# Winograd convolution: the weights' load moved from SyncE's to ScalarE's hardware queue

## The chip, the cores and the metric

The kernel runs on one core of a Trainium2 chip. The metric is the device time of one execution in microseconds (us), told as the median of several runs. Beside it a profiled execution gives a span (first to last instruction, some 1.8 us shorter than the time) and a trace of every instruction and every DMA packet. In the lines of the profile PE is TensorE's matrix unit and PEld its loading of weights, DVE is VectorE, ACT ScalarE, POOL GpSimd, SP SyncE; a q behind the name is the engine's sequencer, which issues transfers, and L48 is line 48 of the kernel.

## The reference

A 3x3 convolution with padding 1, in float32: 16 images of 64 channels and 64 x 64 pixels, 128 output channels.

```python
x_pad = np.pad(x, ((0, 0), (0, 0), (1, 1), (1, 1)), mode='constant')
for b in range(batch):
    for co in range(c_out):
        for ci in range(c_in):
            for kh in range(3):
                for kw in range(3):
                    output[b, co] += weight[co, ci, kh, kw] * x_pad[b, ci, kh:kh+h, kw:kw+w]
```

In are 16.8 MB of images and 0.295 MB of weights, out are 33.5 MB.

## The kernel before

Two images form a pair, one on each half of the partitions; there are 8 pairs. All loads and all stores go out on SyncE's queue, in this order: weights, pair 0 in four pieces, pairs 1 to 6 whole, then the stores pair by pair, with the load of the last pair slipped in after the third store. The weights are cast, transposed on TensorE and combined before the first image matmul can run.

```python
    w_raw = const.tile([CO, CI * 9], F32)
    nc.sync.dma_start(w_raw, w_flat)
    cuts = [(0, 18), (18, 34), (34, 50), (50, 64)]
    # ... cut: buffers of load(p) ...
        for lo, hi in cuts if p == 0 else [(0, H)]:
            keep(
                nc.sync.dma_start(
                    xf[p][:, lo:hi, :], x_rows[128 * p : 128 * p + 128, lo:hi, :]
                )
            )
    # ... cut ...
    for p in range(LATE):            # LATE = 7
        load(p)
    # ... cut ...
    keep(nc.vector.tensor_copy(w16, w_raw))
    # ... cut: 18 transposing matmuls of w16 into wps[1], wps[2], wps[0] ...
    keep(nc.scalar.copy(wrow(G1), wps[1]))
    sums(nc.vector, 0, xf[0], 0, RB)
    # ... cut: main loop over pairs and blocks of 8 row pairs ...
            parts = {3: (0, 64)} if p < NP - 1 else {1: (0, 32), 3: (32, 64)}
            if blk in parts:
                lo, hi = parts[blk]
                keep(nc.sync.dma_start(
                    out_pairs[p, :, :, lo:hi, :],
                    ots[p].rearrange("p b j i c -> p b (j i) c")[:, :, lo:hi, :],
                ))
                if p == 2:
                    load(LATE)
```

## Time and profile before

| | before |
|---|---|
| median time | 127.7 us (127.53 to 127.8) |
| span of the profiled execution | 126.6 us |
| PE, VectorE, ScalarE busy | 106.0, 84.3, 65.5 us |
| DMA packets | 50.77 MB, mean 401 GB/s |
| last store issued | 112.84 us |

Two more views matter for this change. First, the page's DMA issues (what, queue, count, KB each, median us from issue to landing):

```profile
xf<-in_x_dram SPq DMA_DIRECT2D x1, 576.0 KB, 4.9
...
w_raw<-in_weight_dram SPq DMA_DIRECT2D x1, 288.0 KB, 3.0
```

Second, the timeline of the head (start us, us, engine, line, operation, and in brackets the idle time before it and what ended it):

```profile
3.72 0.46 DVE L88 CAST w<-w_raw 128x576 f16<-128x576 f32 x1 [3.72 <-DMA w_raw<-in_weight_dram]
...
4.90 0.48 ACT L118 CAST Wt<-wp 128x384 f16<-128x384 f32 x1 [2.88 <-PE wp L116]
...
6.06 0.69 DVE L98 TENSOR_TENSOR ss<-xf 128x512 f16<-128x512 f32 x1 [1.88 <-DMA xf<-in_x_dram]
...
6.80 1.47 PE L174 MATMUL acc<-ss,Wt 64*128 64x512 f16 x6 [1.24 <-DVE ss L98]
```

The reader is to see that the first weight row is ready at 4.90 + 0.48 = 5.38 us, and that the first matmul then waits until 6.80 for the image's row sum: in the kernel before, the image is the later of the two.

### The profile page before, as it was taken

Reading aid. Unit: us, or ns where it says so; the run is one execution under the profiler, and the core shown is the slowest. Engines: PE = TensorE matmul, PEld = TensorE weight load, DVE = VectorE, ACT = ScalarE, POOL = GpSimd, SP = SyncE. Lnnn points to the kernel's source line nnn. Section 1 sums busy time; section 2 is a strip of 40 time slices with the busy share of each in tenths; the row PEclk is TensorE's granted clock in tenths of the full one; section 3 lists DMA queues with packets and bytes.
Section 4 is the critical chain, followed back from the end, with each engine's and each line's share of the span. In section 5 each row is a group of like instructions: output and inputs, shape, how many; then the busy total and the mean of one; then the engine's idle time right before and its main releaser. Section 6 shows DMA issues by size and latency. Waiting matters only on the chain.

```text
span 126.6 us, 2424 instructions
## 1 busy us (share of the span) xinstructions
PE 106.0 (84%) x978; PEld 55.8 (44%) x978; DVE 84.3 (67%) x135; ACT 65.5 (52%) x98; POOL 33.3 (26%) x22
## 2 busy tenths in 40 slices
PE   0489999999999999999999999999999999920000
PEld 0334555555555555555555555555555555500000
DVE  0287777777777777777877787778777877760000
ACT  4283999998789876666333333336666333300000
POOL 2000395930780075007600660068000000000000
PEclk9999999999999999999999999999999999999555
DMA  4999999999999999999999999999999999999940
GB/s 116 322 422 435 424 430 419 450 419 424 430 440 437 409 442 409 435 435 419 440 414 435 424 419 435 430 435 430 414 430 445 424 424 419 432 417 424 432 184 13
DMA packets 4186, 50.77 MB, mean 401 GB/s; under 512 B 336, under 2 KB 336, under 8 KB 976
## 3 DMA queue, kind: packets, MB, share of 16 engines
q1 hardware_dynamic: 4176, 50.63, 95.1%
q8 instruction: 7, 0.11, 0.3%
q14 instruction: 3, 0.02, 0.0%
HBM read 17.07 MB, written 33.55 MB: 400 GB/s over the span
## 4 chain that ended last, share of the span: by engine, by line
PE 82%; DMA 4%; DVE 2%; issue 1%; DVEq 0%; SPq 0%
PE acc L174 82%; DMA xf<-in_x_dram 4%; DVE ot L194 1%; DVE ss L98 1%; DVEq L230 0%; DVE ot L197 0%; SPq L48 0%; DVEq L194 0%
## 5 line engine op out<-in xcount | busy, mean ns | idle before, releaser
L174 PE MATMUL acc<-xs,Wt 64*128 64x504 f16 (+3 forms) x768 | 88.9, 378 | 0.0
L174 PEld LDWEIGHTS <-Wt 64*128 64x128 f16 x960 | 54.7, 95 | 50.9 <-issue 3.3
L194 DVE TENSOR_TENSOR ot<-acc,ut 128x512 f32<-128x512 f32 x64 | 41.2, 686 | 21.9 <-PE acc L174 18.2
L188 ACT COPY ut<-acc 128x512 f32<-128x512 f32 x64 | 34.4, 590 | 39.7 <-issue 35.2
L197 DVE TENSOR_TENSOR ot<-acc,ut 128x512 f32<-128x512 f32 x64 | 41.1, 683 | 0.2 <-PE acc L174 0.2
L75 ACT CAST xs<-xf 128x1024 f16<-128x1024 f32 (+2 forms) x30 | 30.9, 1065 | 0.7 <-DMA xf<-in_x_dram 0.7
L174 PE MATMUL acc<-ss,Wt 64*128 64x504 f16 (+1 forms) x192 | 27.1, 384 | 1.2 <-DVE ss L98 1.2
L98 POOL TENSOR_TENSOR ss<-xs 128x1024 f16<-128x1024 f16 x8 | 16.8, 2124 | 30.8 <-PE acc L174 30.8
L98 POOL TENSOR_TENSOR ss<-xf 128x1024 f16<-128x1024 f32 x6 | 14.1, 2363 | 23.5 <-DMA xf<-in_x_dram 14.9
L116 PE MATMUL wp<-ident,w 128*64 128x128 f16 x18 | 1.3, 329 | 4.2 <-DVE w L88 4.2
L98 DVE TENSOR_TENSOR ss<-xf 128x512 f16<-128x512 f32 x4 | 2.8, 689 | 2.8 <-DMA xf<-in_x_dram 2.8
L116 PEld LDWEIGHTS <-w 128*64 128x64 f16 x18 | 1.1, 211 | 4.2 <-DVE w L88 4.2
L88 DVE CAST w<-w_raw 128x576 f16<-128x576 f32 x1 | 0.5, 460 | 3.7 <-DMA w_raw<-in_weight_dram 3.7
L118 ACT CAST Wt<-wp 128x384 f16<-128x384 f32 x1 | 0.5, 479 | 2.9 <-PE wp L116 2.9
L75 POOL CAST xs<-xf 128x896 f16<-128x896 f32 x2 | 1.9, 926 | 0.0
L118 ACT ACT_TABLE_LOAD x1 | 1.3, 1283 | 0.7 <-PEq L219 0.7
L123 ACT CAST Wt<-wp 128x384 f16<-128x384 f32 x1 | 0.5, 479 | 0.5 <-DVE Wt L121 0.5
L120 DVE TENSOR_TENSOR Wt<-wp,Wt 128x384 f16<-128x384 f32 x1 | 0.6, 550 | 0.0
L121 DVE TENSOR_TENSOR Wt<-wp,Wt 128x384 f16<-128x384 f32 x1 | 0.5, 547 | 0.0
L124 ACT CAST Wt<-wp 128x384 f16<-128x384 f32 x1 | 0.5, 485 | 0.0
masks.py:199 POOL TENSOR_SCALAR_AFFINE_SELECT ident<-ident 128x128 f16<-128x128 f16 x1 | 0.3, 295 | 0.1
masks.py:197 POOL MEMSET ident<- 128x128 f16 x1 | 0.2, 205 | 0.3 <-POOLq L219 0.3
(4 smaller groups left out, 0.4 us busy)
## 6 DMA issues: line engine op xcount, KB each, us to landing
out_dram<-ot SPq DMA_DIRECT2D x7, 4096.0 KB, 21.1
xf<-in_x_dram SPq DMA_DIRECT2D x7, 2048.0 KB, 21.2
out_dram<-ot SPq DMA_DIRECT2D x2, 2048.0 KB, 13.6
xf<-in_x_dram SPq DMA_DIRECT2D x2, 512.0 KB, 6.1
xf<-in_x_dram SPq DMA_DIRECT2D x1, 576.0 KB, 4.9
xf<-in_x_dram SPq DMA_DIRECT2D x1, 448.0 KB, 7.2
w_raw<-in_weight_dram SPq DMA_DIRECT2D x1, 288.0 KB, 3.0
```

The source lines that it names most:

```text
L75: keep(copy(xs[p][:, lo:hi, :], xf[p][:, lo:hi, :]))
L88: keep(nc.vector.tensor_copy(w16, w_raw))
L98: eng.tensor_add(ss[p][:, lo : lo + n, :], v[:, lo : lo + n, 0, :], v[:, lo : lo + n, 1, :])
L116: nc.tensor.matmul(wp[q : q + 64, k * CO : k * CO + CO], w16[:, t::9], ident)
L118: keep(nc.scalar.copy(wrow(G1), wps[1]))
L120: keep(nc.vector.tensor_sub(wrow(G21), wps[2], wrow(G1)))
L121: keep(nc.vector.tensor_sub(wrow(G01), wps[0], wrow(G1)))
L123: keep(nc.scalar.copy(wrow(G0), wps[0]))
L174: nc.tensor.matmul(tiles[b2][:, lo - j0 : hi - j0, c_lo:c_hi], Wt[p0 : p0 + 64, wi, kw, :], rhs, start=i == 0, stop=i == n - 1,)
L188: keep(nc.scalar.copy(ut, U[b2]))
L194: nc.vector.tensor_add(ots[p][:, b2, j0 : j0 + RB, 0, :], A[b2], us[b2])
L197: nc.vector.tensor_add(ots[p][:, b2, j0 : j0 + RB, 1, :], Bt[b2], us[b2])
```

## The change

Its intent: SyncE's first instruction becomes the first image load, which therefore is issued earlier, and the weights come beside it on the other hardware queue. The whole diff:

```diff
     w_raw = const.tile([CO, CI * 9], F32)
-    nc.sync.dma_start(w_raw, w_flat)
+    nc.scalar.dma_start(w_raw, w_flat)
```

## The prediction

> **What bounds the kernel now.** I read four views, in this order: the 40 slices of the page, the chain that ended last, the DMA issues asked one by one, and the DMA view of the last 11.6 us. The slices come first, because they show which resource has no idle slice. The three rows are tenths of VectorE busy, tenths of DMA busy, and GB/s; a slice is 126.6 / 40 = 3.165 us.
>
> ```profile
> DVE  0287777777777777777877787778777877760000
> DMA  4999999999999999999999999999999999999940
> GB/s 116 322 422 435 424 430 419 450 419 424 430 440 437 409 442 409 435 435 419 440 414 435 424 419 435 430 435 430 414 430 445 424 424 419 432 417 424 432 184 13
> ```
>
> The reader is to see that the transfers fill every slice but the first and the last two, at some 428 GB/s (the table of stretches has 427 to 429 in each 20 us from 5 to 105 us), and that they go on for nearly three slices after VectorE has stopped. The page counts 50.77 MB; 50.77 MB / 428 GB/s = 118.6 us of a span of 126.6. So the DMA engines are the candidate, although the chain of waits puts 82% on the matmuls. The chain's own rows show why that is no contradiction (start us, us, what):
>
> ```profile
> 0.74 0.39 SPq L48
> ...
> 1.19 4.85 DMA xf<-in_x_dram
> ...
> 6.06 0.70 DVE ss L98
> ...
> 6.80 103.47 PE acc L174 x948
> ...
> 112.22 0.60 DVE ot L197
> ```
>
> It ends at 112.8 us, when the last output half is computed; 13.8 us follow in which nothing computes. Line 201's last store is issued at 112.84 and takes 12.8 us to land, although its 2048 KB (2.10 MB) need only 2.10 / 428 = 4.9 us at the steady rate. The other 7.9 us it stands behind older stores. Asked issue by issue, the 4 MB stores (9.8 us of transfer each) issued at 87.23, 100.04 and, 2 MB, at 106.39 took 18.6, 15.8 and 14.3 us: they landed about 105.8, 115.8 and 120.7, so each next store was issued 5.8 to 9.4 us before the one ahead of it had landed. The queue never runs empty.
>
> The DMA view of 115 to 126.6 us (slices of 0.29 us) shows who is last:
>
> ```profile
> DMA  9899999999999989999666655110000000000000
> GB/s 395 339 452 452 452 452 452 452 424 395 395 452 452 424 367 424 452 424 452 283 254 282 254 254 226 57 56 28 28 28 28 28 28 0 28 0 0 0 0 0
> ```
>
> From about 122.8 us to 125.2 only some 28 GB/s flow, close to a sixteenth of 428 (26.8): one of the 16 engines is still working alone. The page's queue list offers a cause:
>
> ```profile
> q8 instruction: 7, 0.11, 0.3%
> ```
>
> These are seven packets of 16 KB that fetch instructions. 0.3% of 16 x 126.6 us is 6.1 us, 0.9 us each. If one engine carries them all, it falls behind the others, whose rate in this view begins to drop at about 120.5, by some 4 to 6 us, which fits. The trace view doesn't name engines, so this identity is inferred. What sets the end is then **the slowest DMA engine**: its first packet, its fixed load of bytes and fetches, whatever it loses in the head, and some 1.4 us after it has ended.
>
> **What the Trainium skill says.** "DMA: Bandwidth & Descriptors", section "Issuing engines are not separate DMA queues": DMAs of scalar, sync or gpsimd run on the same 16 engines and interleave; issuing from several "will only save the time on the sequencer it takes to initiate the DMA, which is usually small relative to the DMA itself." The trace of before has one issuing queue and can't show the interleaving, but it gives the sequencer's time: 0.39 us for the weights. Same page, "Queues, rings and completion order": each engine takes turns between the rings it has work for, a packet at a time. No run here shows that yet; I use it below for where the weights land. "ScalarE: Activation LUTs", section "What ACT_TABLE_LOAD costs": a table load takes about 1283 ns; the trace agrees, one of 1283 ns from 0.74 to 2.02 us. It matters because the weights' issue may have to stand before or behind it.
>
> **The change part by part.**
>
> Removed: the weights' issue on SyncE, 0.74 to 1.13 us (0.39 us; with the gap the first image piece follows at 1.19). So the ten image issues, which take 6.43 us from 1.19, move up by 1.19 - 0.74 = 0.45 us. The 11th, and all stores, wait for computation or for buffers, not for that.
>
> Added: one issue on ScalarE's queue, about 0.4 us. ScalarE's first cast is at 4.90 us, and its table load ends at 2.02, so 2.9 us lie free there. If the table load stays behind the issue (I take 3 in 4, since the load is booked on line 118, after the weights' line), the issue goes out at 0.74 as before; if ahead, at about 2.02, 1.28 us late.
>
> Moved in time, DMA: not one byte is removed. The first packets before started in the slice at 1.75 us, 1.0 us after the first issue began at 0.74. After, some issue also begins at 0.74, so the engines' work starts at the same 1.75 us. The 0.45 us is sequencer time only; it is hidden because each engine has work queued: the second image issue of before went out between 1.6 and 2.0 us, while the weights and first piece (295 + 590 KB, 2.1 us at 428 GB/s) kept the engines busy to at least 1.75 + 2.1 = 3.8 us.
>
> What can be won is only head inefficiency. From 0 to 10 us the view of DMA counted 2.90 MB, worth 2.90 / 428 = 6.8 us at the steady rate, so of 10 - 1.75 = 8.25 us some 1.45 us were lost to slow early packets. Two queues with packets of two transfers side by side might hide part of these first latencies. I choose a seventh, **0.2 us**; nothing in the trace measures it.
>
> Moved in time, computation: the weights now share the engines with the 590 KB first piece. If engines alternate row by row (2304 B and 4608 B, 128 rows each), the weights are done about when the first piece is, not at 3.72 but near 5.5 to 6.0 us; the first piece lands about where it did, 5.6 to 6.1 instead of 6.04. From the weights' landing to the first weight row takes 3.72 to 4.90 + 0.48 = 5.38, 1.66 us. From 5.5 to 6.0 that gives 7.2 to 7.7 us for the first matmul, against 6.80: **0.4 to 0.9 us later**, with the weights in the place of the image as what the first matmul waits for. VectorE's program order supports this, as the weights' cast stands ahead of the first row sum. With the table load ahead it could be 1 us or more.
>
> That delay costs nothing at the end: all stores shift by it, and the tightest queue is the store of 100.04 us. The one before it landed at 105.8, 5.8 us later; less the 1.0 us from issue to first packet, some 4.8 us of delay would fit on the slowest engine. By the same token a gain in computation wouldn't shorten the end either.
>
> Sum: 127.7 - 0.2 (head) + 0.0 (computation) = **127.5 us**.
>
> **Rivals.** First, that the matmuls are the bound, as the 82% of the chain suggest. Then an image piece 0.45 us earlier would start the matmuls at 6.35 and end at 127.25, or the late weights would push it to 128.1 to 128.6. Against it: the 13.8 us after the last computation and the 12.8 us of a store that needs 4.9. Second, that the head of the queue moves as a whole: all packets after the weights 0.45 us earlier, also 127.25. Against it: the same first packet time and engines fed without gaps. Third, that two queues overlap the slow first packets and win back much of the 1.45 us, to some 126.5. For it: the first half microsecond moves just 100 to 200 GB/s and idle slots appear there. Against it: later packets of the first piece, with a full queue behind them, are slow too (the GB/s row of slices stays at 322 to 6.3 us). Fourth, that alternating rings cost something per packet: at most a few tenths, as the weights are 128 of some 4,180 packets.
>
> **Range and chances.** The runs of before span 127.53 to 127.80, so noise is about 0.15 each way. Head gains of 0 to 0.7 us and losses up to 0.4 give 126.9 to 128.0. A change by 2% is 2.55 us: faster would need more than the whole 1.45 us lost in the head, slower would need computation 4.8 + 2.55 = 7.4 us late; I give 1% to each and 98% to the same.
>
> **What would show it right or wrong.** Right: the DMA slices full as before with the first packets at about 1.75 us; the weights landing near the first image piece, at 5 us or later; the chain's first piece a wait for the weights and the matmuls starting after 7 us; the last computation later by the same amount while the last store lands within 0.5 us of before; one engine alone at 28 GB/s at the end. Wrong in a step: first matmul at or before 6.8 (no sharing row by row), or first packets before 1.6 us. Wrong as a whole: if the instruction fetches fell differently, on several engines, the 2 to 4 us of the lone engine would shrink and the time could fall by over 2%; or if a store found its queue empty, a late start would count in full.

## The result, and the profile after

| | before | after |
|---|---|---|
| median time, 6 runs each | 127.69 us (127.40 to 127.80) | 127.69 us (127.43 to 127.86) |
| ratio | | 1.0002, interval 0.9985 to 1.0019 |
| first image matmul | 6.80 us | 8.10 us |
| last store issued | 112.84 us | 113.45 us |
| span of the profiled execution | 126.6 us | 125.7 us |

A ratio is the mean time of one kernel's runs over the mean of the other's in the same rounds, so it isn't quite the ratio of the medians quoted. Executions over 1.5% slower than the fastest of the same kernel are left out of the means. The two spans differ by more than the times do; single executions scatter by that much (the profiled one of before took 128.41 us, where the median is 127.69), so the difference of the spans is not read as a gain.

The slices of the page after (tenths of DMA busy, and GB/s):

```profile
DMA  3999999999999999999999999999999999999970
GB/s 73 367 425 438 438 427 412 427 438 438 427 433 417 414 435 438 438 427 417 422 438 427 443 412 417 438 433 427 438 422 422 433 417 417 425 417 430 425 305 13
```

The same picture as before: no slice between the head and the tail is free. The page's queue list shows the weights' 0.29 MB on a queue of their own (q10), and still seven instruction packets:

```profile
q1 hardware_dynamic: 4032, 50.33, 94.7%
q10 hardware_dynamic: 144, 0.29, 0.9%
q8 instruction: 7, 0.11, 0.3%
```

The issues of the page, to be held against the two lines shown of before:

```profile
xf<-in_x_dram SPq DMA_DIRECT2D x1, 576.0 KB, 5.4
...
w_raw<-in_weight_dram ACTq DMA_DIRECT2D x1, 288.0 KB, 5.6
```

And the timeline of the head:

```profile
0.73 0.39 ACTq L48 DMA_DIRECT2D w_raw<-in_weight_dram  x1
...
0.74 6.94 SPq L63 DMA_DIRECT2D xf<-in_x_dram  x10
...
1.15 1.28 ACT L118 ACT_TABLE_LOAD   x1 [1.15 <-PEq L219]
6.33 0.46 DVE L88 CAST w<-w_raw 128x576 f16<-128x576 f32 x1 [6.33 <-DMA w_raw<-in_weight_dram]
...
8.10 1.46 PE L174 MATMUL acc<-ss,Wt 64*128 64x512 f16 x6
```

The image load is issued 0.45 us earlier (0.74 instead of 1.19) but lands at 0.74 + 5.4 = 6.1 us, where it landed before. The weights are issued when they were, and land 2.6 us later: at 6.31 instead of 3.72. So the weights are now what the first matmul waits for, and it starts 1.3 us later. Of these 1.3 us the last store sees 0.61 (112.84 to 113.45), as the matmul stretch of the chain shortened from 103.47 to 102.71 us: the first 24 matmuls of cast image rows took 4.13 us before and 3.41 us after. No wait stands between them in either trace. Single matmuls of line 174 are longer at first, 0.57 to 0.63 us each until 10.9 us before and 10.6 us after, against 0.38 us from then on, and 20 of them ran in that slow stretch before, 12 after. Why it is slow, no run here shows. The end of the kernel sees nothing of all this.

The DMA view of 115 to 125.7 us after, in slices of 0.27 us, again ends with one engine alone at 28 GB/s:

```profile
DMA  9999999999999999899996542000000000000000
GB/s 424 424 452 424 424 452 424 452 396 395 452 424 424 452 424 452 367 424 452 424 424 283 226 198 113 28 28 28 28 28 28 0 0 0 0 0 0 0 0 0
```

### The profile page after: what moved, and what is told of

The parts are those of the page before. It is cut to its first block, busy times and chain, and to the rows that moved or that the text cites. A ratio compares the mean times of both kernels' runs of the same rounds, so it can differ in the third digit from the quotient of the medians.

```text
span 125.7 us, 2424 instructions
## 1 busy us (share of the span) xinstructions
PE 105.2 (84%) x978; PEld 48.0 (38%) x978; DVE 84.1 (67%) x135; ACT 65.4 (52%) x98; POOL 33.4 (27%) x22
## 4 chain that ended last, share of the span: by engine, by line
PE 83%; DMA 4%; DVE 1%; issue 1%; DVEq 0%
PE acc L174 82%; DMA w_raw<-in_weight_dram 4%; PE wp L116 1%; DVE ot L194 1%; DVE ot L197 0%; DVEq L230 0%; DVE w L88 0%; DVEq L194 0%
## 5 line engine op out<-in xcount | busy, mean ns | idle before, releaser
L174 PE MATMUL acc<-xs,Wt 64*128 64x504 f16 (+3 forms) x768 | 87.7, 376 | 0.0
L174 PEld LDWEIGHTS <-Wt 64*128 64x128 f16 x960 | 46.9, 95 | 56.8 <-issue 1.0
L174 PE MATMUL acc<-ss,Wt 64*128 64x504 f16 (+1 forms) x192 | 26.6, 384 | 0.0
```

What stands on the lines that cost most here:

```text
L174: nc.tensor.matmul(tiles[b2][:, lo - j0 : hi - j0, c_lo:c_hi], Wt[p0 : p0 + 64, wi, kw, :], rhs, start=i == 0, stop=i == n - 1,)
```

## The experiments

The theory to test: the DMA engines, and of them the slowest, set the end; the computation has slack in front of its stores. The rival: the matmul chain sets the end, and here a gain of 0.45 us and a loss happened to cancel.

**1. Start the computation later still: weights behind two pieces of pair 0.** From the changed kernel, the weights' load was taken out of its place and put on SyncE's queue:

```diff
-    nc.scalar.dma_start(w_raw, w_flat)
...
+            if p == 0 and lo == 18:          # behind the second piece
+                keep(nc.sync.dma_start(w_raw, w_flat))
```

> The weights go back to SyncE's queue, behind the first two image pieces (1.11 MB), so the computation should start later than in either kernel: weights landing about 7.3 us, first image matmul about 9.2 us against 6.8 before and 8.1 after. Theory (the slowest DMA engine sets the end, computation has about 4.8 us of slack on it): time within 0.4 us of before, 127.3 to 128.1. Rival (the matmul chain sets the end): 2.4 us more, about 130.1.

Measured: 127.58 us, ratio to before 0.9990 (0.9966 to 1.0014). The first matmul started at 8.85 us, the last store was issued at 115.27, 2.4 us later than before, and the time is the same. The matmul chain's 130.1 us did not come: this much delay of the computation is hidden.

**2. Weights behind all of pair 0** (`if p == 0 and hi == H`). It ran after experiment 3, to find where hiding ends.

> The weights stand behind the four pieces of pair 0 on SyncE's queue. From the runs with the weights behind two pieces (first image matmul 8.9 us) and behind pair 1 (19.7 us), the first image matmul should come at about 11.2 us, 4.4 later than before. Theory as mended by those runs: the end is the later of two, the slowest DMA engine (about 125 us whatever the computation does) and the store issued at 100 us in the kernel before plus some 20.5 us for it and the two half stores; the second gives 104.5 + 20.5 = 125.0, plus up to 1 us of lag and 1.4 us to the end of the span. So the knee: 127.7 to 129.0. Rival (the matmul chain alone): 132.0.

Measured: 129.72 us (128.68 to 130.03), ratio 1.0156 (1.0116 to 1.0196), some 2.0 us more, for a last store issued 4.0 us later (116.85). That is above the expected range: the profiled execution was the fastest of its five and fits (128.68 us), the other four took 129.44 to 130.03. Why they did is open.

**3. Weights behind pair 1** (`if p == 1`).

> The weights stand behind pairs 0 and 1 on SyncE's queue, so they land near 15 us and the first image matmul starts near 17 us, some 10 us later than before. That is more than the 4.8 us of slack. Theory: the stores find the queue empty and the end moves by 10 less about 5, so 131.5 to 133. Rival (matmul chain): by the whole 10 us, about 137.7.

Measured: 137.61 us, ratio 1.0756 (1.0723 to 1.0789), 9.65 us more. My number was missed, since the start came later than I had worked out: first matmul at 19.74 us and not 17, last store issued at 126.62, 13.8 us later than before. That the rival's 137.7 came out is a coincidence: it stood for a delay of 10 us that counts in full, and here 9.65 of 13.8 us counted and 4.1 were hidden. The timeline shows what the start lost:

```profile
14.27 4.87 POOL L99 TENSOR_TENSOR ss<-xf 128x1024 f16<-128x1024 f32 x2 [12.96 <-DMA xf<-in_x_dram]
14.92 2.00 DVE L89 CAST w<-w_raw 128x576 f16<-128x576 f32 x1 [14.92 <-DMA w_raw<-in_weight_dram]
16.84 2.84 DVE L99 TENSOR_TENSOR ss<-xf 128x512 f16<-128x512 f32 x1
```

The same cast takes 0.46 us in the other kernels and the same row sum 0.68; here both fell under GpSimd's two row sums of pair 1 (14.27 to 19.14 us) and took 2.00 and 2.84 us. The Trainium skill, "SBUF — State Buffer", section "SBUF: two separate sides", says that GpSimd and some operations of VectorE, those with two SBUF inputs among them, share a port pair under an exclusive lock, held for the whole instruction. The trace agrees with that in time, though no run here takes GpSimd's work away to prove it.

Read together, the profiled executions of 1 to 3 and of experiment 5 give a rule that the prediction lacked. The distance from the issue of the last half store to the end of the span:

| kernel | last store issued | span | distance |
|---|---|---|---|
| before | 112.84 | 126.6 | 13.8 |
| after | 113.45 | 125.7 | 12.2 |
| weights behind two pieces | 115.27 | 125.8 | 10.5 |
| weights behind pair 0 | 116.85 | 126.9 | 10.0 |
| weights behind pair 1 | 126.62 | 136.7 | 10.1 |
| last pair not loaded | 112.88 | 123.0 | 10.1 |

The distance falls until it meets a floor of about 10.1 us, and from there on the end moves with the computation. So the end is the later of two: the slowest DMA engine, near 125.7 to 126.6 us in this load, and the last store plus about 10.1 us. Each row is one profiled execution; other spans of the same kernels reach 128.3 us behind pair 0 and go down to 135.4 behind pair 1, and where their last stores stood isn't recorded, so the floor is known to 1 us or so. Before, it leaves 13.8 - 10.1 = 3.7 us of slack in the profiled execution, which was a long one; at the more usual span of 125.8 us it is 2.9 (an estimate), and the timed runs of experiment 2 give 4.0 - 2.0 = 2.0 us.

**4. A third of the matmuls.** Only the middle column of the taps is multiplied; the result is wrong, the transfers are the same.

```diff
-                n = 3 * len(wi_rows)
+                n = len(wi_rows)
-                    for kw in (1, 0, 2):
+                    for kw in (1,):
```

> Only the middle column of the taps is multiplied (wrong result on purpose): a third of the matmuls, the same transfers. Theory (DMA engines set the end): at most the few us by which the last engine trails the others are saved, 123 to 128 us; if the trailing comes from fetching the matrix instructions, nearer 123.5, and fewer instruction packets than 7 on queue 8. Rival (matmul chain): PE work falls from 103 to some 35 us and the time to VectorE's 85 us or so, about 95 to 105 us.

Measured: 125.76 us, ratio 0.9846 (0.9822 to 0.9871). PE's last busy slice is the 30th of 40, that is before 93.1 us, and for 28 us the DMA engines work alone at full rate:

```profile
PE   0078868899978999888888874987930000000000
...
DMA  3999999999999999999999999999999999999991
```

PE was busy for 72.2 us and not for the expected 35, as the granted clock, the share of TensorE's full clock that the chip allowed, was 0.77 on average (0.96 before). Even so the last store was issued at 94.0 us, 19 us earlier than before. The chain of matmuls is refuted as the bound: two thirds of the matmuls taken away saved 1.5%.

**5. 2.1 MB less to transfer.** The last pair is not loaded, its computation uses the pair before. Its output is wrong, which doesn't matter for the time.

```diff
-                    load(LATE)
+                    xf[LATE] = xf[LATE - 1]
```

> The last pair is not loaded but computed from the pair before it (wrong result on purpose): 2.10 MB of 50.77 fewer, the same computation. Theory: the slowest engine has 2.10 MB / 428 GB/s = 4.9 us less to do, and about 4.8 us of slack at the store of 100 us would be used up, so between 3 and 5 us faster, 122.7 to 124.7. Rival (matmul chain): no change, 127.7.

Measured: 125.46 us (124.81 to 126.11), ratio 0.9823 (0.9777 to 0.9870), 2.3 us less. The direction is the theory's and the rival's "no change" fails, but the size is below what I expected. The stretches 95 to 98 and 98 to 101 us (length, busy of PE, PEld, VectorE, ScalarE, GpSimd with counts, granted clock, DMA share, GB/s) show where the rest went:

```profile
95.00:98.00 3.00, 3.00 (x32) 1.30 (x30) 2.27 (x5) 1.77 (x4) 0.00 (x0) 1.00 0.89 377
98.00:101.00 3.00, 3.00 (x32) 1.36 (x30) 2.42 (x5) 1.23 (x3) 0.00 (x0) 1.00 0.14 55
```

The DMA engines ran dry before the store that is issued at 100.07 us: 55 GB/s instead of 428. With 4.9 us of transfers removed, the computation became the bound, at the floor of 10.1 us.

**6. Who shares what in the head: shorter rows.** The first piece of pair 0 in four transfers of 4, 4, 4 and 6 image rows, so that a partition's row is 1024 or 1536 B long and not 4608.

```diff
-        for lo, hi in cuts if p == 0 else [(0, H)]:
+        for lo, hi in [(0, 4), (4, 8), (8, 12), (12, 18)] + cuts[1:] if p == 0 else [(0, H)]:
```

> As the changed kernel, but the first image piece (18 rows) comes in four transfers of 4, 4, 4 and 6 image rows, so a row of a transfer is 1024 B and not 4608 B. Theory (an engine takes turns packet by packet, a packet being one row of a transfer): the weights' 128 rows go out beside 128 rows of 1024 B, so they are done after 426 KB and not 885 KB, and land at 4.5 to 5.2 us instead of 6.3; first image matmul at about 7 us. Rival (the queues share by bytes): they land as in the changed kernel, within 0.4 us of 6.3. Time the same either way, 127.4 to 128.0.

**7. Longer rows.** Pair 0 in one transfer, rows of 16384 B (one run, state unknown).

```diff
-        for lo, hi in cuts if p == 0 else [(0, H)]:
+        for lo, hi in [(0, H)]:
```

> As the changed kernel, but pair 0 comes in one transfer with rows of 16384 B. Packet by packet: the weights are done after 128 x (2304 + 16384) B = 2.4 MB, landing at about 7.5 to 8.5 us. By bytes: landing near or before 6.3 us, as the two queues would still give equal shares. The computation starts at about 10 us as pair 0 is whole; the time stays within 0.6 us of before.

Measured for both, the weights' issue line of each page, first with the short rows, then with the long:

```profile
w_raw<-in_weight_dram ACTq DMA_DIRECT2D x1, 288.0 KB, 3.4
```

```profile
w_raw<-in_weight_dram ACTq DMA_DIRECT2D x1, 288.0 KB, 8.5
```

The same 288 KB issued at 0.73 us take 3.4, 5.6 and 8.5 us to land, with nothing changed but how pair 0 is cut in the other queue (first rows of 1024, 4608, 16384 B). Beside short rows the weights landed a little sooner than expected (4.1 against 4.5), beside long ones later (9.2 against 8.5 at most). Shares by bytes are refuted. The packed trace agrees with turns by row: when the last of the weights' 128 rows began, the other queue had begun 211, 189 and 142 rows, roughly one for one, but 0.22, 0.84 and 2.33 MB. The times: 127.77 us, ratio 0.9993 (0.9947 to 1.0038), and 127.97 us, though the first matmuls stood at 7.73 and 11.05 us. With short rows the first matmul waited for the image again, which landed 0.9 us later than before.

**8. Relieve one engine.** The last store in two transfers, of 120 and 8 partitions.

```diff
-                keep(nc.sync.dma_start(
-                    out_pairs[p, :, :, lo:hi, :],
-                    ots[p].rearrange("p b j i c -> p b (j i) c")[:, :, lo:hi, :],
-                ))
+                last = p == NP - 1 and blk == 3
+                for r0, r1 in [(0, 120), (120, 128)] if last else [(0, 128)]:
+                    keep(nc.sync.dma_start(
+                        out_pairs[p, r0:r1, :, lo:hi, :],
+                        ots[p].rearrange("p b j i c -> p b (j i) c")[r0:r1, :, lo:hi, :],
+                    ))
```

> As the changed kernel, but the last 2 MB store is two transfers, of partitions 0 to 119 and 120 to 127. The first should use 15 engines only. If the engine that trails is the sixteenth, its last share is taken from it and the end comes 1 to 2 us sooner, about 126. If it is another engine, 127.5 to 128.5.

Measured: 130.61 us, ratio 1.0205 (1.0146 to 1.0264), slower by more than either guess. The split itself did what was intended: the trace has 15 completion packets of 4 B for the first of the two transfers and 8 for the second, 23 in all, where a store has 16 otherwise. The DMA view of 115 to 128.8 us (slices of 0.345 us) has the rate sinking long before the lone end:

```profile
GB/s 427 451 380 356 332 356 309 332 332 309 261 214 237 214 142 190 261 332 332 214 309 190 166 261 142 237 95 214 214 71 71 95 24 24 24 24 0 0 0 0
```

So the 120-partition store itself went slower, and one engine still trailed. Which engine trails, this run can't say; the try failed.

**9. Are the instruction fetches a part of the lag?** One tap had 338 matmuls instead of 978 and only 2 instruction packets. This kernel has one tap's computation in the original number of instructions: each of its matmuls is cut into three of 2 or 3 rows. Its output is wrong, which doesn't matter for the time. It ran beside a repeat of one tap on the same chip.

```diff
+                            for a, z in [(lo, lo + 3), (lo + 3, lo + 6), (lo + 6, hi)]:
                                 nc.tensor.matmul(
-                                    tiles[b2][:, lo - j0 : hi - j0, c_lo:c_hi],
+                                    tiles[b2][:, a - j0 : z - j0, :],
```

(The operand is cut the same way, and each part is its own accumulation group.)

> As the run with one tap, but each matmul is cut into three of 2 or 3 image rows (wrong result on purpose), so the matrix engine has the changed kernel's number of instructions again and still much less to compute. If the fetching of instructions makes the slowest DMA engine trail: 7 instruction packets on queue 8 again and the lag of the last engine back from 2.2 to 3 us or more, time at 127 us or above. If the trailing and the 1.8 us come from the computation itself being slow: 2 instruction packets or 7, the time stays near the 125.8 us of one tap.

> The run with one tap once more, on the same chip as the one cut in three: 125.8 us within 0.3, with 2 instruction packets on queue 8.

Measured: 127.16 us, ratio 0.9970 (0.9948 to 0.9991), and 126.20 us, ratio 0.9882 (0.9855 to 0.9910). Their queue lists, in this order:

```profile
q8 instruction: 7, 0.11, 0.3%
```

```profile
q8 instruction: 2, 0.03, 0.1%
```

The repeat came out 0.4 us above the first run of one tap. Still, with PE busy 71.1 and 71.9 us, the same computation took (0.9970 - 0.9882) x 127.6 = 1.1 us longer with three times the instructions and five more packets of 16 KB. Of the 1.5 us that one tap gains beside it (0.0118 x 127.6), about three quarters go with the instruction count, the rest with the computation. By its number this is what the expectation said of fetches on the slowest engine.

The packed traces say otherwise. They hold each packet's start, length and size, and an engine's 16 KB store packet starts 4 ns before the one ahead of it ends; with the number of rows that each transfer gives an engine, each of the 16 engines can be followed back from its last packet to 24 us. In the kernel before, the six fetches after 24 us then lie on six different engines, which end at 122.1 to 122.4 us; the engine that ends last, at 125.17, carries none. What it has is slow packets: its 16 KB store packets take 644 ns (median) from 41 to 112 us, while the computation runs, and 611 elsewhere, as on the other engines. Of all the kernel's 104 packets between 625 and 675 ns, 100 are on this engine, together 3.5 us over. With each matmul cut in three it is the same: the last engine has no fetch and 59 slow packets, 2.5 us over. In the two runs of one tap the slow engine is only 1.4 us over and ends at 122.1 and 122.2; an engine with a fetch ends last there, at 122.8 and 123.3. So what grows with the instruction count is one engine's slow packets, 2.5 us for 1.4, and not fetches on it; that the instructions make them slow is the likely reading, but no run shows the link, and which engine it is stays open.

**10. The changed kernel in five rounds.**

> The changed kernel itself in five rounds, to see whether the 0.2 us expected from the head of the transfers can be seen: 0.2 us is a ratio of 0.998. Its computation starts 1.3 us later, so if the matmul chain counted even in part the ratio would be above 1.003.

Measured: 127.64 us, ratio 1.0005 (0.9988 to 1.0022). Neither 0.998 nor a ratio above 1.003.

## Why the prediction was right

The time, 127.69 us, lies in the range (126.9 to 128.0), and "same" came. By the prediction's steps:

- **The bound is the DMA engines, and the slowest of them.** Right. Experiment 4 took two thirds of the matmuls for 1.5%; experiment 5 took 2.1 MB of transfers for 1.8%. The lone engine at 28 GB/s is there after the change too. The reason given for the lag of that engine is wrong: it carries none of the six fetches that could be followed, which lie on six other engines, and its own store packets are slow, 644 ns for 611 (experiment 9). That the fetches' 4 to 6 us fitted the lag was luck.
- **The 0.45 us of earlier issue is hidden.** Right. The image piece was issued 0.45 us earlier and landed at the same 6.1 us. That all ten image issues move up by 0.45 us was wrong: they took 6.94 us instead of 6.43, so the tenth ended at 7.68 us, against 7.62 before. The DMA view of the first 10 us has its first traffic after the change in the slice at 1.75 us, as before.
- **ScalarE issues first, then loads its table.** Right: 0.73, then 1.15 to 2.43 us.
- **The weights change places with the image as the first matmul's wait.** Right in kind, mis-sized: expected a landing at 5.5 to 6.0 us and a first matmul 0.4 to 0.9 us later; measured 6.31 and 1.3 us. The terms that were short are the landing (0.3 us above the upper end) and the way from there to the matmul (8.10 - 6.31 = 1.8 us for 1.66). That the engines alternate row by row, which the prediction could only take from the skill, experiments 6 and 7 show.
- **The last computation is later by the same amount.** Half wrong: 0.61 us of the 1.3 remained.
- **4.8 us of slack.** Right in its use, too large: 2.9 to 3.7 us by the profiles, 2.0 by the timed runs of experiment 2. The step followed one store to the engine that is latest for it, and left out that after a late store the following two still have to pass, which would make the floor of 10.1 us: an estimate from the store of 100.04 us is 1.0 to the first packet, 8.39 MB / 428 GB/s = 19.6 for the three stores and 1.4 to the end, that is 122.0 us or 9.2 after the last issue, and a lag of one engine of about 0.9 beside it (in the run with the last pair not loaded).
- **0.2 us from the head.** Not found. In the first 10 us 2.95 MB moved instead of 2.90, worth 0.05 / 428 = 0.12 us, but the two ratios, 1.0002 and 1.0005, have intervals that begin above the 0.9984 that 0.2 us would be. The best estimate for this term is zero.

No version that beats both kernels came out of this. The traces say what one would need: relief for the one engine with slow packets, worth at most the 2.0 us before and 1.7 us after by which it ends behind the next engine, and past 2 to 4 us a last store issued earlier, since the floor of the computation is no further away.

## What to carry to other kernels

Here a load issued 0.45 us earlier bought nothing, since the transfer engines had their first packets at the same 1.75 us and enough work from then on; look at the GB/s row before moving a load to another queue. A small transfer put beside a large one on a second queue landed the later, the longer the large one's rows were (3.4, 5.6 and 8.5 us), so a load that must be first is safer ahead of the others in one queue (3.0 us in the kernel before), or beside short rows. And when the chain of waits names one engine but the span goes on long after its last instruction, take work from each candidate separately: a third of the matmuls and a missing load told in two runs which one counts. A number that comes out as expected doesn't prove the reason behind it: experiment 9 gave the time expected of fetches, and the packets show another cause.

## What the Trainium skill lacked or had wrong

- "DMA: Bandwidth & Descriptors", "Queues, rings and completion order", says that an engine changes rings at packet boundaries and calls 9 to 17 descriptors a typical packet; it doesn't say how many rows of a transfer that is. Here the turn was about a single row: landing times of 3.4, 5.6 and 8.5 us beside rows of 1024, 4608 and 16384 B. The page doesn't draw the consequence that a small load's landing depends on the row length in the other queue.
- The same page, "Where 436 GB/s comes from", says that for HBM to SBUF transfers the HBM side, about 358 GB/s, binds. With one core running, the trace has 427 to 429 GB/s in each 20 us from 5 to 105 us, loads and stores mixed. The page itself has 425 GB/s from one core in the same passage, so what the sentence lacks is the condition.
- "Runtime: NRT & Kernel Launch", "Instruction fetch mechanics", calls the cost of crossing a 16 KiB block of instructions mostly hidden; it doesn't say what it costs a kernel that is bound by its transfers. Here each 16 KB instruction packet kept one transfer engine for 0.88 to 1.01 us (kernel before).
- No page that I read explains an engine that trails when all transfers are hardware-issued: it worked alone for some 2.0 us before and 1.7 us after the change, with store packets of 644 ns for 611 while the computation ran. Which engine it is, and why, stays open.
